# A small early read of b on ScalarE's queue, and one store moved to GpSimd's queue, in a two-product GELU kernel

## The chip, the cores and the metric

The kernel runs on one core of a Trainium2 chip. The metric is the device time of one execution in microseconds; before the change it is 120.03 us (median of 3 runs, 119.86 to 120.13). The profile covers one execution with a span of 118.1 us, from the first to the last instruction; TensorE's granted clock is 1.00 throughout.

## The reference

```python
m, k, n, p = 1024, 1024, 2048, 1024          # a: m x k, b: k x n, c: n x p, all float32
h = np.matmul(a, b)
h = 0.5 * h * (1 + np.tanh(np.sqrt(2 / np.pi) * (h + 0.044715 * h ** 3)))
return np.matmul(h, c)
```

Two matrix products with a GELU between them. All inputs and the output are float32 in HBM; the kernel computes the products in bfloat16 and, for sums of blocks, in a rounded float32.

## The kernel before, in words

The kernel keeps everything on chip: a (transposed), b, the hidden matrix h (transposed, as the left operand of the second product) and c. The order of instructions on each engine is the order in which the program writes them (a manual schedule); completion of loads and stores is signalled over semaphores that are handed out in turn, eight for the transfers issued by SyncE and ScalarE and eight for those issued by GpSimd.

**Loads.** SyncE issues the first twelve loads of 512 KB each (L67 to L80). `load_a(h, q)` (L68) brings rows 512h to 512h+511 of a, columns 256q to 256q+255, into the staging tile `sta`. `load_b(q)` (L72) brings rows 256q to 256q+255 of b, columns 0 to 511, into the staging tile `stb`. The order is a(0,0), b(0), a(1,0), and then a(0,q), b(q), a(1,q) for q of 1 to 3. Rows of b are 8 KB apart in HBM, so the first load, b(0), takes 2 KB from each of the rows that make up the first 2 MB of b. GpSimd then loads the rest of b and all of c with a cast to bfloat16 (L87 to L93), six and eight loads; a one-element copy on GpSimd (`gate`, L82) holds these back until a(0,3) has landed. ScalarE runs a dummy GELU (L83) at the start, so that the function table is loaded early.

**First part.** For the first four column tiles of h the product is plain. Each quarter of a half of a is cast to bfloat16 by VectorE or ScalarE (`cast_a`, L117), transposed by TensorE against an identity (`turn`, L125, matmuls of L129), and copied from PSUM into `aT` by VectorE (L131). ScalarE casts b's slices from `stb` to `b1` (`cast_b`, L133 and L136). TensorE multiplies as the pieces come (`mm1`, L103), with stirring matmuls on a zero tile before (`stir`, L114). The order of this first part is written out by hand (L211 to L267).

**Seven products.** The remaining column tiles of h (`zero`, `one`) and the whole second product (`two`) use Winograd's form of Strassen's scheme: seven block products in place of eight (`seven`, L286, matmuls of L194), with sums and differences of blocks on VectorE (L152), plain copies on ScalarE (L184, L190), PSUM snapshots on ScalarE (L278) and additions on VectorE (L283).

**Stores.** In the second product every finished 128-row piece of the output goes through `done2` (L405) to `store` (L402, L403) on SyncE's queue. Those of the upper left quarter (`(i, l) == (0, 0)`) leave in two halves of 256 columns. The pieces pass through the tile `ot` of a pool with four buffers, tag "o" (L282). The last two pieces are made at L349 and stored from L350.

Of the kernel before, what the change touches and what calls it, by code (L numbers as in the profile page):

```python
# [9 lines left out]
F32 = mybir.dt.float32  # L10
# [9 lines left out]
def kernel(ctx, tc, a, b, c, out):  # L20
    nc = tc.nc
# [3 lines left out]
    H = 512  # L25
# [8 lines left out]
    consts = ctx.enter_context(tc.tile_pool(name="consts", bufs=1))  # L34
# [11 lines left out]
    def pieces(tag, bufs, shape, dt, name):  # L46
        return small.tile(shape, dt, name=name, tag=tag, bufs=bufs)
# [19 lines left out]
    def load_a(h, q):  # L67
        nc.sync.dma_start(out=sta[q // 2][:, h, q % 2],  # L68
                          in_=av[:, 4 * h:4 * h + 4, ds(q * 256, 256)])

    def load_b(q):
        nc.sync.dma_start(out=stb[:, 2 * q:2 * q + 2], in_=bv[:, 2 * q:2 * q + 2, 0:H])  # L72

    load_a(0, 0)
    load_b(0)
    load_a(1, 0)
    for q in range(1, 4):
        load_a(0, q)
        load_b(q)
        load_a(1, q)  # L80
# [7 lines left out]
    for n in range(2):  # L88
        for k in range(0, KT, 4):
            nc.gpsimd.dma_start(out=b2[:, k:k + 4, ts(n, H)],  # L90
                                in_=bv[:, k:k + 4, ds(1024 + n * H, H)])
# [310 lines left out]
    def store(mt, q0, w, ot, eng=None):  # L402
        (eng or nc.sync).dma_start(out=out[ts(mt, 128), ds(q0, w)], in_=ot)  # L403

    def done2(i, l, j, p):  # L405
        if (i, l) == (1, 0):
            ot = pieces("o", 4, [128, H], F32, "ot")
            nc.vector.tensor_copy(ot, p)
            p = ot
        n = 2 if (i, l) == (0, 0) else 1  # L410
        for q in range(n):
            r = ds(q * (H // n), H // n)
            store(4 * i + j, l * H + q * (H // n), H // n, p[:, r])

    def between2(n):
        if n == "P1":
# [11 lines left out]
        elif n == "P73":  # L428
            two.t4(two.t[1], 4)

    seven(two, done2, between2)


# [28 lines left out]
```

## Time and profile before

| | |
|---|---|
| Time | 120.03 us |
| Span of the profile | 118.1 us |
| TensorE busy | 111.9 us (95%) |
| VectorE / ScalarE / GpSimd busy | 90.5 / 58.7 / 11.0 us |
| HBM read / written | 20.97 / 4.19 MB |
| Loads of a by SyncE, 8 of 512 KB: issue to landing, median | 9.1 us |
| Loads of b by SyncE, 4 of 512 KB: issue to landing, median | 8.7 us |
| Stores by SyncE, 12 of 256 KB and 8 of 128 KB: median | 2.1 and 2.0 us |

How to read it: the busy share is an average over stages with different limits, so the chain of waits is read beside it: it goes back from the last instruction to what released each step. In a line of the timeline or of the groups, the last bracket gives the idle time of the engine before the instruction and what ended it; in the windows each line is a stretch of the span with the busy time of each engine, the clock, the mean busy share of the 16 DMA engines and what they moved. A matmul's end is modelled, and a wait for several semaphores is put down to the latest.

### The profile page before, as it was taken

To read this page: it belongs to the slowest core of one execution; us is meant where nothing else is said; L and a number is where in the kernel's file an instruction comes from. 1 tells how busy PE (TensorE), PEld (TensorE's weight loads), DVE (VectorE), ACT (ScalarE), POOL (GpSimd) and SP (SyncE) were. 2 spreads that over 40 slices of the span, in tenths; PEclk is the share of its full clock that TensorE was granted. 3 is DMA by queue.
4 is the path that set the end of the run, shared out by engine and by line. 5 is a ranking of instruction groups with operands and counts; after the bars stand their busy time and mean duration, and the time that the engine had idled before them with its cause. 6 is when DMAs were issued, how large, how long until landed. Compare 5 with 4: busy or idle time off the path is not lost.

```text
span 118.1 us, 1469 instructions
## 1 busy us (share of the span) xinstructions
PE 111.9 (95%) x535; PEld 77.1 (65%) x540; DVE 90.5 (77%) x104; ACT 58.7 (50%) x96; POOL 11.0 (9%) x21
## 2 busy tenths in 40 slices
PE   5998899999998999999999999999999999999980
PEld 5654346544866545888887444588888888888860
DVE  0243697796996899772779999999999986964670
ACT  5046756899767689246679347800042992000000
POOL 2000007952223100000000000000000000000000
PEclk9999999999999999999999999999999999999999
DMA  3999999999999999999000000061000002014993
GB/s 88 289 371 366 366 354 305 177 205 207 205 206 213 211 212 212 211 211 212 15 0 0 0 6 0 0 221 45 0 0 0 0 0 92 3 39 175 364 350 137
DMA packets 13542, 17.91 MB, mean 152 GB/s; under 512 B 736, under 2 KB 8928, under 8 KB 13536
## 3 DMA queue, kind: packets, MB, share of 16 engines
q0 software_dynamic: 5344, 7.34, 35.2%
q1 hardware_dynamic: 8192, 10.49, 26.1%
q8 instruction: 4, 0.07, 0.2%
q14 instruction: 2, 0.02, 0.0%
HBM read 20.97 MB, written 4.19 MB: 213 GB/s over the span
## 4 chain that ended last, share of the span: by engine, by line
PE 80%; DMA 8%; DVE 5%; SPq 2%; issue 1%; ACT 1%; ACTq 0%; DVEq 0%
PE ps L194 69%; PE ps L103 8%; DMA sta<-in_a_dram 8%; DVE x L152 4%; PE pt L129 2%; SPq L68 1%; DVE ot L283 1%; ACT ab L97 1%; SPq L72 1%; DVE ot L349 0%; ACTq L97 0%; DVEq L283 0%
## 5 line engine op out<-in xcount | busy, mean ns | idle before, releaser
L194 PE MATMUL ps<-x,s 128*128 128x512 f32 x128 | 29.6, 391 | 0.0
L194 PEld LDWEIGHTS ps<-x,s 128*128 128x128 f32 x128 | 24.0, 188 | 5.1
L194 PE MATMUL ps<-x,x 128*128 128x512 f32 x96 | 22.9, 394 | 0.0
L194 PEld LDWEIGHTS ps<-x,x 128*128 128x128 f32 x96 | 18.0, 188 | 3.9
L103 PE MATMUL ps<-aT,b 128*128 128x512 bf16 x62 | 15.0, 379 | 0.7 <-DVE aT L131 0.5
L278 ACT ACTIVATE v<-ps 128x512 f32<-128x512 f32 x10 | 6.0, 598 | 17.8 <-PE ps L194 17.8
L194 PE MATMUL ps<-c_sb,hT 128*128 128x512 bf16 (+1 forms) x70 | 14.1, 355 | 0.1
L194 PE MATMUL ps<-x 128*128 128x512 f32 x56 | 13.5, 395 | 0.3 <-DVE x L152 0.3
L194 PEld LDWEIGHTS ps<-x 128*128 128x128 f32 x56 | 10.2, 188 | 3.3 <-DVE x L152 0.8
L107 ACT ACTIVATE hT<-ot 128x512 bf16<-128x512 f32 x18 | 10.7, 625 | 3.3 <-DVE ot L283 3.3
L283 DVE TENSOR_TENSOR ot<-ps,v 128x512 f32<-128x512 f32 x10 | 6.7, 687 | 6.4 <-DMA out_dram<-ot 3.9
L194 PEld LDWEIGHTS <-hT 128*128 128x128 bf16 x72 | 6.9, 98 | 7.0 <-issue 0.5
L194 PE MATMUL ps<-aT,b 128*128 128x512 bf16 x47 | 10.6, 379 | 0.1
L283 DVE TENSOR_TENSOR ot<-ps,u 128x512 f32<-128x512 f32 x10 | 6.7, 689 | 5.2 <-ACT u L278 5.2
L103 PEld LDWEIGHTS <-b 128*128 128x128 bf16 x64 | 5.8, 97 | 6.8 <-DVE aT L131 1.0
L131 DVE COPY aT<-pt 128x512 bf16<-128x512 bf16 x16 | 6.0, 419 | 5.2 <-PE pt L129 5.2
L152 DVE TENSOR_TENSOR x<-c_sb 128x1024 fp32r<-128x1024 bf16 x8 | 9.2, 1216 | 0.0
L194 PEld LDWEIGHTS <-b 128*128 128x128 bf16 x48 | 4.6, 98 | 5.7 <-issue 0.3
L152 DVE TENSOR_TENSOR x<-b 128x1024 fp32r<-128x1024 bf16 (+1 forms) x4 | 7.0, 1752 | 1.0 <-DMA b<-in_b_dram 1.0
L107 ACT ACTIVATE hT<-ps 128x512 bf16<-128x512 f32 x14 | 7.3, 596 | 0.5 <-PE ps L103 0.5
L278 ACT ACTIVATE u<-ps 128x512 f32<-128x512 f32 x10 | 5.8, 596 | 3.4 <-PE ps L194 3.2
L97 ACT ACTIVATE ab<-sta 128x512 bf16<-128x512 f32 (+1 forms) x7 | 5.0, 747 | 4.9 <-DMA sta<-in_a_dram 4.9
(39 smaller groups left out, 111.8 us busy)
## 6 DMA issues: line engine op xcount, KB each, us to landing
sta<-in_a_dram SPq DMA_DIRECT2D x8, 512.0 KB, 9.1
c_sb<-in_c_dram POOLq DMA_DIRECT2D x8, 512.0 KB, 19.8
b<-in_b_dram POOLq DMA_DIRECT2D x6, 512.0 KB, 10.9
out_dram<-ot SPq DMA_DIRECT2D x12, 256.0 KB, 2.1
stb<-in_b_dram SPq DMA_DIRECT2D x4, 512.0 KB, 8.7
out_dram<-ot SPq DMA_DIRECT2D x8, 128.0 KB, 2.0
```

The costliest lines, as they stand in the source:

```text
L68: nc.sync.dma_start(out=sta[q // 2][:, h, q % 2], in_=av[:, 4 * h:4 * h + 4, ds(q * 256, 256)])
L72: nc.sync.dma_start(out=stb[:, 2 * q:2 * q + 2], in_=bv[:, 2 * q:2 * q + 2, 0:H])
L97: nc.scalar.activation(dst, src, AF.Copy)
L103: nc.tensor.matmul(p, b1[:, k, ts(t, 128)], aT[:, h, k], start=(k == 0), stop=(k == KT - 1))
L107: nc.scalar.activation(hT[h][:, t], p, AF.Gelu_apprx_tanh)
L129: nc.tensor.transpose(pt[:, n, ts(m, 128)], ab[:, m, ts(n, 128)], ident)
L131: nc.vector.tensor_copy(aT[:, h, 2 * q + n], pt[:, n])
L152: nc.vector.tensor_tensor(out=dst[:, r], in0=x[:, r], in1=y[:, r], op=op)
L194: nc.tensor.matmul(p[:, ds(c0, w)], l[:, k, ts(j, 128)], r[:, k, ds(c0, w)], start=(start and k == 0), stop=(k == self.kt - 1), skip_group ...
L278: nc.scalar.activation(st, p, AF.Copy)
L283: nc.vector.tensor_tensor(out=ot, in0=p, in1=st, op=ADD)
```

## The change

A new tile `head` of 32 partitions and 16 float32 each is loaded on ScalarE's queue, ahead of everything else that ScalarE does. It takes the first 64 bytes of rows 0, 8, 16 and so on up to 248 of b: one small read in every 64 KB of the 2 MB from which the first load of b takes its slices. Nothing reads the tile. It is meant to touch b's memory before the large load asks for it. In addition, the first of the twenty stores of the output leaves on GpSimd's queue in place of SyncE's. With one transfer more at the front and one less among the stores, the later stores use the same completion semaphores in the same turns as before.

```diff
@@ -70,6 +70,10 @@
 
     def load_b(q):
         nc.sync.dma_start(out=stb[:, 2 * q:2 * q + 2], in_=bv[:, 2 * q:2 * q + 2, 0:H])
+
+
+    head = consts.tile([32, 16], F32, name="head")
+    nc.scalar.dma_start(out=head, in_=b.rearrange("(r e) n -> r e n", e=8)[0:32, 0, 0:16])
 
     load_a(0, 0)
     load_b(0)
@@ -410,7 +414,9 @@
         n = 2 if (i, l) == (0, 0) else 1
         for q in range(n):
             r = ds(q * (H // n), H // n)
-            store(4 * i + j, l * H + q * (H // n), H // n, p[:, r])
+            first = (i, l, j, q) == (0, 0, 0, 0)
+            store(4 * i + j, l * H + q * (H // n), H // n, p[:, r],
+                  nc.gpsimd if first else nc.sync)
 
     def between2(n):
         if n == "P1":
```

## The prediction

> **What bounds the kernel now.** I read the page first, then the chain of waits in order of time, then the early stretches window by window, then the timelines of ScalarE, VectorE and GpSimd. Busy time alone says TensorE:
>
> ```profile
> PE 111.9 (95%) x535; PEld 77.1 (65%) x540; DVE 90.5 (77%) x104; ACT 58.7 (50%) x96; POOL 11.0 (9%) x21
> ```
>
> The chain shows when that begins to be true (start, length, what):
>
> ```profile
> 0.74 0.44 SPq L68
> ...
> 3.40 9.11 DMA sta<-in_a_dram
> ...
> 12.62 1.16 ACT ab L97 x2
> ...
> 13.82 0.40 PE pt L129 x4
> 14.22 1.51 PE ps L103 x7
> ```
>
> Until 12.5 us the end is set by the stream of input loads, then by one cast of ScalarE, and from 13.8 us almost only by TensorE. Whatever moves the start of that dense stretch moves the end. So the question is how fast the queue of SyncE delivers a and b in the first 12 us. The windows (stretch, its length, busy us of PE, PEld, DVE, ACT, POOL, clock, DMA share, GB/s):
>
> ```profile
> 3.00:3.50 0.50, 0.50 (x3) 0.34 (x2) 0.00 (x0) 0.00 (x0) 0.00 (x0) 1.00 1.08 379
> 3.50:4.00 0.50, 0.50 (x3) 0.41 (x2) 0.00 (x0) 0.00 (x0) 0.00 (x0) 1.00 1.12 385
> 4.00:4.50 0.50, 0.50 (x3) 0.25 (x1) 0.19 (x1) 0.00 (x0) 0.00 (x0) 1.00 1.01 233
> 4.50:5.00 0.50, 0.47 (x2) 0.00 (x0) 0.50 (x1) 0.00 (x0) 0.00 (x0) 1.00 0.83 213
> 5.00:5.50 0.50, 0.44 (x5) 0.44 (x6) 0.00 (x1) 0.00 (x0) 0.00 (x0) 1.00 0.88 225
> 5.50:6.00 0.50, 0.50 (x7) 0.50 (x5) 0.00 (x0) 0.00 (x0) 0.00 (x0) 1.00 0.99 297
> 6.00:6.50 0.50, 0.50 (x3) 0.41 (x3) 0.37 (x2) 0.00 (x0) 0.00 (x0) 1.00 1.06 369
> ```
>
> There is a hole from 4.0 to 6.0 us: 213 to 297 GB/s between stretches of 369 to 385, with the transfer engines still busy (share 0.83 to 1.01). They are not short of work; each packet takes longer. The packet records of the trace say which: the 256 packets of 2 KB of b's first load last 123 ns on average, those of the three later b loads 90 to 91 ns, and the 1 KB packets of a that run beside the end of the first b load, from 5.7 us, keep their usual 46 ns. So the slowness belongs to b's first slice, not to the moment. The first load of a shows a smaller thing of the kind: some packets of 375 to 553 ns at its start, a mean of 52 ns against 46 to 51 later.
>
> Size of the hole: (376-233)+(376-213)+(376-225)+(376-297) = 536 GB/s, times 0.5 us, is 268 KB; at 376 GB/s that is 0.71 us. From the packets: (123-90) ns x 256 / 16 engines = 0.53 us for a mean engine. The arrivals agree (start, length, what, idle before):
>
> ```profile
> 6.63 1.24 ACT L136 ACTIVATE b<-stb 128x256 bf16<-128x256 f32 x3 [4.39 <-DMA stb<-in_b_dram]
> 9.73 1.15 ACT L97 ACTIVATE ab<-sta 128x512 bf16<-128x512 f32 x2 [1.86 <-DMA sta<-in_a_dram]
> 11.04 1.15 ACT L136 ACTIVATE b<-stb 128x512 bf16<-128x512 f32 x2 [0.16 <-DMA stb<-in_b_dram]
> 12.62 1.15 ACT L97 ACTIVATE ab<-sta 128x512 bf16<-128x512 f32 x2 [0.43 <-DMA sta<-in_a_dram]
> ```
>
> VectorE's first cast begins at 4.31 us with the first a load, ScalarE's first b cast at 6.63: 2.32 us for 512 KB, where a later b load needs 1.31 us (9.73 to 11.04).
>
> **What the Trainium skill says.** "DMA: Bandwidth & Descriptors", section "Issuing engines are not separate DMA queues": loads of different engines run on the same 16 transfer engines and interleave. So the small load neither gets its own path nor has to queue behind all of a. The same page, section "Queues, rings and completion order": an engine changes between rows packet by packet; so the small packets can go among a's first ones. No run of before has two queues at once, so the trace can't confirm either. Section "Latency and other measured facts" gives 0.2 us for an HBM access, up to 2 us at high load; the long a packets of 0.38 to 0.55 us lie within that. No page that I found says that a first touch of a tensor is slow; this I infer from the packets alone.
>
> **The change part by part.**
>
> *The small load.* 32 rows of 64 bytes, one in each 64 KB of the first 2 MB of b, which are exactly the rows of b's first load. Nobody reads the tile. Bytes: 2 KB, nothing against 512 KB. Packets: 2 per engine; at 46 ns (a's 1 KB packet, an upper bound when nothing stalls) 0.09 us, at the longest first packet of a, 0.55 us, up to 1.1 us. I take the lower end, because its stall overlaps the start of a's own stream; the upper end goes into the range. Issue: nearest row is SyncE's 0.44 us for the first L68. It stands ahead of ScalarE's table load (0.74 to 2.02 us) and the dummy gelu (to 2.23 us); behind these ScalarE idles 4.39 us until 6.63. 0.44 us, even 1 us, is hidden there.
>
> *What it does for b.* It goes out at about 0.74 us, beside a's first load; b's own packets start at 3.7 us by the packet records. If the slowness is that of a first touch, it is spent before 3.7 us while a streams. Upper bound of the gain 0.71 us (all of the hole), lower bound 0. Not all need be cured: only 32 small reads warn of 256 packets, and engines that fetch a given row need not be those that touched it. I take two thirds of the hole, 0.5 us, which is also about the packets' 0.53.
>
> *Does 0.5 us arrive at the end?* Every load after b's first is in the same queue, so all arrive 0.5 us earlier. The first block of products gains less (its a half is ready only at 6.13 + 0.76 us on VectorE), but the cast that the chain names starts at 12.62 on a landing, with 0.43 us of idle before it, and the 7 products ahead of it end 0.34 us before its transposes start; they too wait for landings (b's cast at 11.04). From then on TensorE is dense, and the later landings and the gate for GpSimd's loads (18.4 us) shift alike. So up to some 0.8 us passes one to one.
>
> *The rotated semaphores.* Loads and stores of SyncE take turns over eight completion semaphores, and the extra load shifts the turns by one. The third b load now waits for the small load. It is issued at 5.43 us; with the 1.9 to 3.5 us that the page's issues take at least to land, the small one lands by about 4.7. Behind that issue stand the last four loads of SyncE, whose data has a backlog: no cost. The other waits keep their partners.
>
> *The first store on GpSimd.* GpSimd's last work:
>
> ```profile
> 37.97 0.71 POOL L93 DMA_DIRECT2D c_sb<-in_c_dram  x1 [1.84 <-DMA b<-in_b_dram]
> ```
>
> It is free at 76.4 us when the store is due; issue by that row some 0.7 us, landing perhaps 1 us later than SyncE's 2.0. The buffer is wanted again when VectorE makes its fifth output, after 96 us. The other 19 stores keep their order and their old semaphores. Cost 0. The last stores stay on SyncE.
>
> Sum: 120.03 - 0.5 + 0.0 = 119.5 us.
>
> **The rivals.** *The hole isn't a first touch.* The first two or three packets of b in every engine are normal (84 ns); the slow ones come after 4.05 us. A first touch would rather hit the first packets, unless reads run ahead of what the records show. Also b's second load touches 2 MB of its own and isn't slow. It could be 16 engines stepping through rows 8 KB apart in step, and falling out of step later. Then the small load mends nothing: 120.0 us.
>
> *The stall is moved, not hidden.* If the small reads block their engine for 0.55 us, as long as a's longest packet, a's first load is late by that; if 0.2 us of the hole is saved: 120.03 + 0.35 = 120.4 us, slower. For it: the same engines serve both. Against it: a's own first packets are stalling then anyway, and b's slow packets cost an engine far less than one serial stall each.
>
> *Overheads of a second hardware queue or of GpSimd's store.* A delay of SyncE's first issue while ScalarE issues too, up to the 0.44 us of one issue, would pass fully to the end: 120.3 us, with half the hole mended 120.1. The store itself can't add.
>
> **How the numbers follow.** Hole mended wholly or partly, 119.1 to 119.75: 0.60, likeliest 119.5. Not mended, no cost: 0.17. Stall moved: 0.15. Overhead: 0.08, mostly slower, a little of it within. Thus faster 0.60, same 0.18, slower 0.22. The range 119.0 to 120.4 takes the full hole plus the 0.2 us by which runs of before differ (119.86 to 120.13) below, and the moved stall above.
>
> **What would show it.** Right: windows of 4 to 6 us at 330 GB/s or more, ScalarE's first b cast near 6.1, the cast of the chain near 12.1, and all of TensorE half a microsecond earlier. If b's first cast still starts 2.3 us after VectorE's first cast, the hole isn't a first touch. If VectorE's first cast moves from 4.31 to 4.6 or later, the stall or the issue delays a. If ScalarE's wait for b no longer ends at a landing, or a TensorE gap appears after 76 us, the part on the store or on ScalarE is wrong.

## The result and the profile after

The changed kernel takes 119.12 us (median of 6 runs, 118.96 to 119.28) against 119.87 us for the kernel before (median of 6 runs, 119.78 to 120.13). The ratio is 0.9934, with a 95% interval of 0.9919 to 0.9949: faster by 0.75 us. Measured a second time beside the kernel before, the whole change gave 0.9925 (0.9905 to 0.9944). The two profiled executions, from which the lines below come, differ by 0.6 us (spans of 118.1 and 117.5 us).

The forecast of 119.5 us lies near, and in direction it was right. Its reason was not. The stretches of the changed kernel that answer to the hole in the load stream (columns as before: stretch, length, busy us by engine, clock, DMA share, GB/s):

```profile
4.00:4.50 0.50, 0.50 (x3) 0.25 (x1) 0.00 (x0) 0.00 (x0) 0.00 (x0) 1.00 0.99 268
4.50:5.00 0.50, 0.47 (x2) 0.00 (x0) 0.30 (x1) 0.00 (x0) 0.00 (x0) 1.00 0.97 229
5.00:5.50 0.50, 0.05 (x1) 0.05 (x2) 0.40 (x1) 0.00 (x0) 0.00 (x0) 1.00 0.90 233
5.50:6.00 0.50, 0.50 (x6) 0.50 (x7) 0.00 (x0) 0.00 (x0) 0.00 (x0) 1.00 0.93 320
```

The hole is still there: 229 to 320 GB/s where it was 213 to 297. The packets of b's first load last 123.8 ns on average, before 123.4. ScalarE's timeline after says the same (start, length, what, idle before):

```profile
0.74 0.45 ACTq L76 DMA_DIRECT2D head<-in_b_dram  x1
1.22 1.28 ACT L87 ACT_TABLE_LOAD   x1 [1.22 <-PEq L452]
2.51 0.20 ACT L87 ACTIVATE g<-warm 128x1 f32<-128x1 f32 x1
6.82 1.24 ACT L140 ACTIVATE b<-stb 128x256 bf16<-128x256 f32 x3 [4.10 <-DMA stb<-in_b_dram]
9.68 1.15 ACT L101 ACTIVATE ab<-sta 128x512 bf16<-128x512 f32 x2 [1.62 <-PE pt L133]
10.94 1.15 ACT L140 ACTIVATE b<-stb 128x512 bf16<-128x512 f32 x2
12.37 1.15 ACT L101 ACTIVATE ab<-sta 128x512 bf16<-128x512 f32 x2 [0.28 <-DVE aT L135]
```

The first b cast is not earlier, it is 0.19 us later (6.82 for 6.63). The small read landed 2.5 us after its issue at 0.74, thus at 3.2 us and ahead of b's first packets, and did not help. The cast at 12.37, however, is 0.25 us earlier. Its load, a(1,1), lands at 12.27 us, before at 12.51, and the cast follows 0.10 to 0.11 us later in both. The line after names VectorE's copy, which ends at 12.34, but the distance to the landing is the same as before, so the load sets this moment here too, or nearly so. The time is gained behind the first b load. The same window of ten microseconds, of before and then of after:

```profile
8.00:18.00 10.00, 8.92 (x65) 4.47 (x66) 6.71 (x12) 5.65 (x9) 0.00 (x0) 1.00 1.08 363
```

```profile
8.00:18.00 10.00, 9.28 (x70) 4.84 (x70) 6.62 (x12) 5.98 (x11) 0.31 (x2) 1.00 1.07 394
```

The stream runs at 394 GB/s in place of 363, at the same DMA share. The packet records say how. From a's fourth load on, which starts at about 9.5 us, a's packets of 1 KB last exactly 46 ns each after the change, and 49.8 to 51.3 ns on average before; in the three later loads of b the packets of 2 KB last 84 ns each, before 90.0 to 90.8 on average. The second load of a shows no such difference: 46.2 ns before, 46.9 after. Nothing in the diff speaks of these transfers.

How it comes to the end is seen in three places. GpSimd's gate, which waits for a(0,3), of before and of after:

```profile
18.42 0.18 POOL L82 COPY gate<-sta 128x1 f32<-128x1 f32 x1 [17.12 <-DMA sta<-in_a_dram]
```

```profile
17.69 0.18 POOL L86 COPY gate<-sta 128x1 f32<-128x1 f32 x1 [16.38 <-DMA sta<-in_a_dram]
```

VectorE's first sum over b's second half, which GpSimd's loads bring, of before and of after:

```profile
27.81 1.23 DVE L152 TENSOR_TENSOR x<-b 128x1024 fp32r<-128x1024 bf16 x1 [1.03 <-DMA b<-in_b_dram]
```

```profile
27.20 1.22 DVE L156 TENSOR_TENSOR x<-b 128x1024 fp32r<-128x1024 bf16 x1 [0.77 <-ACT hT L111]
```

The line after names ScalarE. But GpSimd's second load of b lands at 27.52 us before and at 26.91 after, 0.29 us ahead of the sum in both, and GpSimd's next load, which waits for a landing of b, starts with the sum in both (27.80 and 27.19). So the sum waits for GpSimd's loads in both kernels.

And the chain of waits after:

```profile
13.98 1.51 PE ps L107 x7
...
25.83 3.47 PE ps L198 x16
29.30 0.03 issue
29.33 0.02 DVEq L287
29.35 0.25 issue
29.60 1.28 DVE ot L287 x2
30.88 4.55 DVE x L156 x4
35.43 0.04 issue
35.47 3.72 PE ps L198 x15
...
75.11 39.09 PE ps L198 x180
114.20 0.02 issue
114.23 0.42 DVE ot L353
```

The middle of it in the chain of before:

```profile
26.18 3.47 PE ps L194 x16
29.64 0.03 issue
29.67 0.02 DVEq L283
29.69 0.52 issue
30.21 1.28 DVE ot L283 x2
```

In the chain of before, the same pieces begin at 14.22, 26.18, 30.21, 36.09, 75.72 and 114.84 us. TensorE's dense stretch starts 0.24 us earlier, and is 0.35 us ahead at 25.83; behind it the wait for VectorE (listed as "issue"; VectorE is still at its sums over b) is 0.25 us in place of 0.52, and from 29.60 on everything is 0.61 us ahead, to the last instruction. So the gain has two steps: 0.35 us from the earlier loads of SyncE, and 0.26 us from the earlier gate and GpSimd's loads behind it. Nothing more is gained or lost after 36 us.

### The profile page after: what moved, and what is told of

The parts are those of the page before. It is cut to its first block, busy times and chain, and to the rows that moved or that the text cites. A ratio compares the mean times of both kernels' runs of the same rounds, so it can differ in the third digit from the quotient of the medians.

```text
span 117.5 us, 1471 instructions
## 1 busy us (share of the span) xinstructions
PE 111.2 (95%) x535; PEld 76.6 (65%) x540; DVE 90.1 (77%) x104; ACT 58.7 (50%) x96; POOL 11.6 (10%) x22
## 3 DMA queue, kind: packets, MB, share of 16 engines
HBM read 20.97 MB, written 4.19 MB: 214 GB/s over the span
## 4 chain that ended last, share of the span: by engine, by line
PE 83%; DVE 6%; DMA 5%; ACT 1%; issue 1%; SPq 0%; DVEq 0%
PE ps L198 70%; PE ps L107 11%; DMA stb<-in_b_dram 5%; DVE x L156 4%; PE pt L133 3%; DVE ot L287 1%; DVE aT L135 1%; ACT ab L101 1%; SPq L68 0%; DVE ot L353 0%; ACT b L140 0%; DVEq L287 0%
## 5 line engine op out<-in xcount | busy, mean ns | idle before, releaser
L282 ACT ACTIVATE p<-ps 128x512 f32<-128x512 f32 x9 | 5.4, 599 | 3.8 <-PE ps L198 3.8
```

What stands on the lines that cost most here:

```text
L282: nc.scalar.activation(st, p, AF.Copy)
```

## The experiments

**Which part does it.** The suspects: the read itself (touch); the place of the tiles in SBUF, since the 64 bytes per partition of `head` push every later tile by 64 bytes (placement); the store on GpSimd or the turns of the semaphores; or the chip on which the profile was taken.

The kernel before, unchanged, as a profile beside the others:

> The kernel before, unchanged, for a profile beside the others on one chip. If the faster load stream of the changed kernel is the change's own doing, b's later loads again last 90 ns a packet and the gate on GpSimd starts at 18.4 us. If it was the chip or the hour, the packets of this run last 84 ns as well and the gate starts near 17.7 us. Ratio to before 1.000 either way.

Ratio 0.9985 (0.9954 to 1.0015). b's later packets last 89.0 to 90.7 ns and a's 49.5 to 51.3, the gate comes at 18.83 us. So the faster stream comes with the change, not with the hour or the chip of the first profile.

The small read alone (the changed kernel with every store on SyncE):

```diff
-            first = (i, l, j, q) == (0, 0, 0, 0)
-            store(4 * i + j, l * H + q * (H // n), H // n, p[:, r],
-                  nc.gpsimd if first else nc.sync)
+            store(4 * i + j, l * H + q * (H // n), H // n, p[:, r])
```

> The small read on ScalarE alone, all stores on SyncE. Theory touch (the read itself does it): 0.993 to 0.994, as the whole change. Theory placement (the 64 bytes of the new tile shift all later tiles): the same. Theory store or turns (the store on GpSimd, or the turns of the semaphores, does it): 0.999 to 1.001.

Ratio 0.9962 (0.9945 to 0.9980): faster, but less so than the whole change. Packets of 46.0 and 84.0 ns, gate at 17.61 us, and VectorE's last sum starts at 114.00 us, as early as in the whole change (114.23). What is missing lies behind that; see the tail below.

The store alone, added to the kernel before:

```diff
+            first = (i, l, j, q) == (0, 0, 0, 0)
+            store(4 * i + j, l * H + q * (H // n), H // n, p[:, r],
+                  nc.gpsimd if first else nc.sync)
```

> The first store on GpSimd alone, no small read and no tile. Touch and placement: 0.999 to 1.001. Store or turns: 0.993 to 0.997.

Ratio 1.0000 (0.9972 to 1.0027), packets of 49.6 to 51.3 and 89.6 to 90.7 ns, as before.

The tile without the read, and with every store on SyncE:

```diff
-    nc.scalar.dma_start(out=head, in_=b.rearrange("(r e) n -> r e n", e=8)[0:32, 0, 0:16])
+    nc.gpsimd.memset(head, 0.0)
```

> The tile of 64 bytes per partition is there and is cleared once by GpSimd, which is idle then; nothing is read from b ahead, stores as before. Touch: 0.999 to 1.001. Placement: 0.993 to 0.994, with b's later packets at 84 ns and a's at 46.

Ratio 0.9893 (0.9851 to 0.9936), median 119.01 us: the whole gain, without reading a byte of b. The window from 8 to 18 us of this kernel shows the fast stream:

```profile
8.00:18.00 10.00, 9.36 (x72) 4.83 (x71) 6.63 (x13) 5.98 (x10) 0.37 (x2) 1.00 1.08 394
```

Touch falls, placement stands. In the compiled programs the staging tiles `stb` and `sta`, and all other large tiles, start at 448 modulo 512 bytes before the change (448 bytes past a multiple of 512 in their partition) and at 0 after it.

**The read with the old placement.** The whole change (read and moved store), and an unused tile that brings the later tiles back to 448 modulo 512:

```diff
+    pad = consts.tile([32, 112], F32, name="pad")
+    nc.gpsimd.memset(pad, 0.0)
```

> The small read with its 64-byte tile, and a second, unused tile of 448 bytes per partition (cleared once by GpSimd), so that all later tiles lie 512 bytes further: the same place modulo 512 as before the change (448). Placement theory: the packets of the later loads are back at 50 ns (a) and 90 ns (b), the gate at 18.4 us or later, ratio 0.998 to 1.003. Touch theory (the read itself helps): 0.993 to 0.995.

Ratio 1.0006 (0.9987 to 1.0024). The window of this kernel:

```profile
8.00:18.00 10.00, 8.99 (x66) 4.52 (x66) 6.71 (x12) 5.66 (x9) 0.00 (x0) 1.00 1.08 364
```

All that the diff shows is in this kernel, and nothing is gained. The gate is back at 18.44 us, a's packets at 49.8 to 51.2 ns. This is the clearest single run of the study.

**Which boundary.** Two unused tiles of other sizes, no read, stores as before (`[32, 80]` and `[32, 48]` in place of `[32, 112]`):

> No small read; one unused tile of 320 bytes per partition: the later tiles start at 256 modulo 512. Placement theory: if a boundary of 256 bytes is what counts, clean packets of 46 and 84 ns and 0.991 to 0.995; if only 512 counts, 50 and 90 ns and about 1.000.

> No small read; one unused tile of 192 bytes per partition: the later tiles start at 128 modulo 512. Placement theory: with a boundary of 128 bytes 46 and 84 ns and 0.991 to 0.995, with one of 256 or more 50 and 90 ns and about 1.000.

At 256 modulo 512: 0.9936 (0.9910 to 0.9961), packets of 46.0 and 84.0 ns. At 128: 0.9996 (0.9976 to 1.0016), 49.7 to 51.7 and 88.9 to 90.7 ns. The windows of the two kernels, in this order:

```profile
8.00:18.00 10.00, 9.36 (x69) 4.69 (x68) 6.61 (x12) 6.08 (x10) 0.00 (x0) 1.00 1.07 394
```

```profile
8.00:18.00 10.00, 8.94 (x66) 4.44 (x66) 6.70 (x12) 5.65 (x9) 0.00 (x0) 1.00 1.09 364
```

Of the four places tried modulo 512, the two that are multiples of 256 are fast (0, 256), the other two slow (128, 448). GpSimd clears the unused tile in the slow kernels as well, so the clearing is not what helps.

**Whose accesses.** Only the staging tiles moved, and the small buffers behind them:

```diff
+    pad = slot("pad", [32, 16], F32, "pad")
+    nc.gpsimd.memset(pad, 0.0)
     stb = slot("x0", [128, KT, H], F32, "stb")
```

> No small read; an unused tile of 64 bytes between b2 and stb, so that only the staging tiles of the float32 loads (and the small buffers after them, the output pieces among these) move to 0 modulo 512, while c, h, aT, b1 and b2 stay at 448. If the placement acts through the writes of SyncE's loads: 46 and 84 ns and 0.991 to 0.995, as with all moved. If it acts through the engines' own reads and writes of b1, aT and h: 50 and 90 ns and about 1.000.

Ratio 0.9933 (0.9908 to 0.9959), 46.0 and 84.0 ns: the whole gain. c, h, aT, b1 and b2 may stay where they were. What moved are the staging tiles and the small buffers, and the packets that changed are those of SyncE's loads into the staging tiles; so it acts through the tiles that these loads write (the small buffers were not moved alone). VectorE's cast of a staged piece lasts 0.69 us and ScalarE's pair of casts 1.15 us before and after, so these reads don't feel it. GpSimd's loads, which cast to bfloat16 on the way, don't show it either: their packets of 1 KB last 99.4 ns before and 100.0 after, those of 2 KB 173.3 and 173.2, though c, b1 and b2 moved with the rest in the whole change.

The Trainium skill has a rule of this kind, in "DMA: Bandwidth & Descriptors", section "How a descriptor splits into AXI transactions": a descriptor (the order to move one piece, here taken as one row of 1 or 2 KB) is cut into transactions of up to 256 bytes that begin at multiples of 256, and where it doesn't start on such a boundary, the first transaction begins at the boundary below, with bytes that are fetched and not used. An estimate by that account: 2 KB from 448, which is 192 modulo 256, are 9 transactions in place of 8, and 1 KB is 5 in place of 4. The page speaks of reading; here the misplaced side is the SBUF destination of the loads. The measured price is smaller than one transaction in eight or four: 90.5 for 84 ns (8%) and 50.4 for 46 (10%). The stores, which read misplaced buffers in SBUF, show some of it too: 48.2 ns a packet of 1 KB before and 45.9 after, 87.5 and 84.2 for 2 KB. That the cut into transactions is the cause isn't shown here; the dependence on 256 is. Nor is the misplaced start enough by itself: a's second load, and GpSimd's loads, show no price at 448. What else it takes stays open.

**The tail, and what the moved store is for.** The read alone lost part of the gain behind the last sum. SyncE's instructions of the closing sequence from the last store's landing on (duration, first and last start), of the read alone and then of the whole change:

```profile
L461 SPq EVENT_SEMAPHORE  x10: 17/28/28, 116.4 to 117.6; - x10
```

```profile
L463 SPq EVENT_SEMAPHORE  x3: 17/17/28, 116.6 to 117.4; - x3
```

At the end SyncE waits for the eight completion semaphores one after the other, some 61 ns apart by the instruction records. In the whole change, as before, the last store signals the last of the eight; the other seven waits are over by then. With the extra transfer and no store moved, the last store signals the first of the eight, and seven waits come after it: 7 x 61 ns = 0.43 us (the medians of the two kernels, 119.52 and 119.12 us, differ by 0.40). From the last landing to the end of the span it is 117.7 - 116.4 = 1.3 us for the read alone, and 117.5 - 116.6 = 0.9 us for the whole change. The last kernel below, which also has an early read and all stores on SyncE, again takes 1.3 us from the last landing (115.95) to the end (117.28). So the moved store pays for the turn that the read costs. The tile alone has no extra transfer, needs no moved store, and shows three such records, as the whole change does.

**The hole, which is still open.** Both on top of the tile without the read, with stores as before. First the two first loads of b exchanged:

```diff
-    load_b(0)
+    load_b(1)
...
-        load_b(q)
+        load_b(0 if q == 1 else q)
```

> The 64-byte tile without the small read, and the first two loads of b change places: rows 256 to 511 are loaded second in the queue, rows 0 to 255 fifth. If the slow first slice is a matter of these addresses, the 2 KB packets of the fifth load last some 124 ns and those of the second 84 ns. If it is a matter of b's first load, whichever rows, or of the place in the queue, the second load has 124 ns and the fifth 84 ns. The kernel itself must be some 3 us slower, since the first products then wait for the fifth load (near 11 us in place of 6.7).

One execution: 124.41 us beside 119.98. The first b load, now rows 256 to 511, has 122.1 ns a packet, and rows 0 to 255, now loaded second, 84.0. The rows don't matter. (The time is 4.4 us up: the first b cast starts at 10.72, and TensorE's granted clock fell to 0.5 in the gap, in the windows from 10 to 12 us.)

Then b's first load ahead of a's:

```diff
-    load_a(0, 0)
     load_b(0)
+    load_a(0, 0)
```

> The 64-byte tile without the small read, and b's first load is issued ahead of a's. If the slowness belongs to b's first load wherever it stands, its packets last some 124 ns from 2.1 us on and a's first packets stay near 52 ns. If it belongs to the second place in the queue, a's first packets are the slow ones (a mean of 65 ns or more) and b's last 84 to 90 ns. Time: VectorE's first cast waits for both loads either way, 0.990 to 1.005 of before.

Ratio 1.0205 (1.0163 to 1.0247), outside what was expected: VectorE's first cast starts at 6.93 us in place of 4.37. b's packets last 143.8 ns, a's after them 47.6. So it is b's first load that is slow, whichever rows it takes and whether it is first or second in the queue.

Last, a touch of every row, with the tiles at 256 modulo 512 and the stores on SyncE (with the tiles at 0 the kernel does not fit: the last pool takes 30 KB per partition, and 29.97 are left):

```diff
-    head = consts.tile([32, 16], F32, name="head")
-    nc.gpsimd.memset(head, 0.0)
+    head = consts.tile([128, 2, 16], F32, name="head")
+    nc.scalar.dma_start(out=head, in_=bv[:, 0:2, 0:16])
+    pad = consts.tile([32, 48], F32, name="pad")
+    nc.gpsimd.memset(pad, 0.0)
```

> The small read made as strong as it can be: 64 bytes from every one of the 256 rows of b's first load, into the same partitions[...]; an unused tile of 192 bytes beside its 128 puts the later tiles at 256 modulo 512. If b's first load is slow because its rows were not touched before, its packets now last 84 to 95 ns, ScalarE's first b cast starts near 6.1 us and the ratio is 0.986 to 0.990. If a touch of any kind does nothing, they last 115 to 130 ns and the ratio is 0.992 to 0.997, since the 256 small packets also lie beside a's first ones.

Ratio 0.9946 (0.9928 to 0.9965), and 113.2 ns a packet: a little under what was expected of a touch without effect, far above a cure, and just under the kernels with this order of loads and no early read, which have 116.4 to 134.6. The first b cast starts at 6.59 us. This read landed 3.6 us after its issue, at 4.3, when b's first load was already running, so it isn't a clean test of an early touch of every row; the changed kernel's own read, which landed at 3.2, is the better one for a touch in time.

The whole change once more:

> The whole change once more, beside the kernel before on this chip. Placement theory: 0.992 to 0.995, with the packets of the later loads at 46 and 84 ns; the small read and the moved store add nothing.

Ratio 0.9925 (0.9905 to 0.9944), 119.18 us, 46.0 and 84.0 ns, and 120.3 ns for b's first load. The unused tile alone had 119.01 us. Their intervals overlap: it is as good as the whole change, with less in it, but not shown to be better.

## Why the prediction was right or wrong

*What bounds the kernel*: right. The load stream of SyncE sets the start of TensorE's dense stretch, and moving it moved the end, by 0.24 us there. *That GpSimd's gate and loads shift alike*: right, and weightier than written, since 0.26 of the 0.61 us come in by way of VectorE's wait for them near 28 us.

*What the small load does for b*: wrong, and this is the step that failed. The slowness of b's first load was measured rightly, but its cause was inferred from the match between the touched rows and the slow load. b's packets went from 123.4 to 123.8 ns; no part of the term of 0.5 us came about. What came in its place is the placement: later packets of 46 and 84 ns for 50 and 90. The prediction had that clue in its own lines, a's packets of "46 to 51" ns and b's later ones of "90 to 91", and took both as usual. The rival "the hole isn't a first touch" described what happened to the hole, and would have been right on the time too (120.0 us) with the old placement: that kernel measured 1.0006.

*The small load costs nothing*: right for its issue (0.45 us, with 4.10 us of ScalarE's idle time left) and its packets. But "nobody reads the tile" was taken to mean that the tile does nothing. A part of the change was not costed at all: its place in SBUF. Put as a term of the sum it can be estimated from the packets. Up to the landing of a(0,3), for a mean engine: the fourth to seventh load of a, 512 packets each, (49.9 + 51.2 + 49.9 + 51.3 - 4 x 46) ns x 32 = 0.59 us, and two loads of b, 256 packets each, (90.0 + 90.6 - 2 x 84) ns x 16 = 0.20 us; together 0.79 us, measured at the gate 0.73.

*The stall is moved, not hidden*: in the profile after VectorE's first cast starts at 4.70 us, 0.39 later than before, which would fit. In the other runs with the small read of 32 rows it is 4.36 to 4.44, without any read 4.19 to 4.47. For the small read no delay is shown; the read of all 256 rows has 4.63, in one profile.

*The rotated semaphores*: right for the whole change, for a reason not seen. Without the moved store the turn would cost 0.43 us at the end. *The first store on GpSimd costs 0*: right (issue 0.56 us, landing 2.3 us; alone 1.0000), but that it pays a cost back was not seen.

*The size*: 0.5 us was forecast and 0.75 measured. The nearness is chance, since neither number contains the other's cause. The test that the prediction itself named would have said so: the hole was to fill to 330 GB/s or more, and ScalarE's first b cast was to start near 6.1 us; neither happened. Two readings on record are off besides. The times at which packets start (3.7, 4.05 and 5.7 us) were read some 0.25 us too late; their durations are right. And before does have two queues at once, for half a microsecond: GpSimd's packets start at 20.12 us and SyncE's last load ends at 20.68. That small packets can go among a's first ones, as the prediction had it, shows after the change: those of the small read run from 2.40 to 2.90 us, and a's first load from 1.85 to 4.33.

## What to carry to other kernels

A new tile, even one that nobody reads, moved here every tile allocated after it; before explaining a gain by what a new instruction does, run the tile without the instruction, and the instruction with the tiles back in place. Put the SBUF tiles that large plain loads write at multiples of 256 bytes per partition: here it was worth 0.7% of the kernel for 64 bytes of padding. The stores' packets grew shorter too, but no time came of that here, and GpSimd's casting loads showed nothing. And an added transfer shifts the turns of the completion semaphores, so look at which of them the last store signals.

## What was not expected of the hardware

In SyncE's loads from about 8 us on, a start of the rows in SBUF at 128 or 448 in place of 0 or 256 (modulo 512) lengthens packets of 1 KB from 46.0 to about 50.4 ns and of 2 KB from 84.0 to about 90.5, and takes the load stream from 394 to 363 GB/s. a's second load, before that, has 46 to 47 ns at 448 too, and GpSimd's loads show no dependence; why isn't shown. On the right boundary packets show no scatter at all once the first loads are through: all of a's from its fourth load on last 46 ns, all of b's later ones 84.

The first load of b takes 113 to 144 ns a packet in every variant, whichever rows it takes and whether it is first or second in the queue, and the first load of a never does so (47.6 to 57.0 ns for 1 KB). An early read of 64 bytes in each 64 KB does not change it. Its cause stays open.
